# One decoder layer on one core: TensorE, ScalarE and VectorE in a written order from the first norm into the up projection, with a new first stage

## The chip, the cores and the metric

The kernel runs on 1 core of a Trainium2 chip. The metric is the device time of one execution in microseconds (us). A core has five engines that run side by side, each through its own list of instructions in order: PE (TensorE, matrix products), DVE (VectorE, elementwise), ACT (ScalarE, activations and copies), POOL (GpSimd, elementwise) and SP (here it only issues DMAs). An instruction waits at the head of its engine's list until what it reads has been written, and everything behind it on that engine waits with it.

## The reference

One layer of a decoder trunk on 1024 prompt tokens and 8 new tokens (1032 rows, width 1024), in float32:

```python
h = rmsnorm(x, w['norm1_w'])
proj = h @ w['w_in']
q_r, f_r, i_r, g_r, z, xbc_r, dt_r = jnp.split(proj, splits, axis=-1)
...
o_a, S_h_new = hgrn2_mix(heads(q), heads(k), heads(i_r.astype(f32)), heads(log_f), S_h.astype(f32))
o_a = rmsnorm(o_a, w['hgrn_norm_w']) * jax.nn.silu(heads(g_r).astype(f32))
...
xbc, buf_s_new = causal_dwconv(xbc_r, buf_s, w['ssm_conv_w'], w['ssm_conv_b'])
xbc = jax.nn.silu(xbc.astype(f32))
...
dt = jax.nn.softplus(dt_r.astype(f32) + w['ssm_dt_bias'].astype(f32))
y, S_s_new = ssd_scan(X * dt[..., None], A * dt, Bh, Ch, S_s.astype(f32))
...
x = x + jnp.concatenate([o_a, y], axis=-1) @ w['w_out']
h = rmsnorm(x, w['norm2_w'])
gate, val = jnp.split(h @ w['w_up'], 2, axis=-1)
gate, buf_f_new = causal_dwconv(gate, buf_f, w['ffn_conv_w'], w['ffn_conv_b'])
x = x + (jax.nn.silu(gate) * val) @ w['w_down']
```

A final norm follows, and all the recurrent and convolution states are written out.

## The kernel before, in words

**Products.** Each float32 operand is split into a rounded high part and the low rest (`wh`, `wl` of a weight, `hh`, `hl` of an activation), and a product is three passes: high by high, low by high, high by low. The input projection runs in jobs of 128 output columns; a job runs over three groups of 344 tokens, each 8 × 3 = 24 products into one of three accumulators of PSUM (`psmm`). A weight tile is read by a DMA into `ws` (512 KB, two buffers), cast to `wh` on ACT and subtracted to `wl` on DVE (`wload`, lines L188 and L189).

**Stages.** First the norm (`first_norm`): ACT squares (L115), root (L117), DVE puts 1/rms on a diagonal `dg` (L119), PE multiplies the token tile `xt` by `dg` into `tp`, which turns it and scales it in one product, ACT evicts the high part (L128) and DVE the low part (L129). Two jobs of the input projection (x8 and x10, the shared B and C) are merged into it, the products for dt follow, then come the other jobs: x0 to x3 and x4 to x7 (columns of x with their causal convolution, `xbc_close`), z0 to z7 (the gate of the state-space group, evicted by ACT as `sz`), and, for eight heads, q, f, i and g (`sg` is the gate's SiLU). Beside the jobs run the state-space scan (`ssd`, 8 chunks for each of two groups, which reads rows of decays from DRAM as `csb` and `ecs` and keeps a state `S`), its 16 decode blocks for the new tokens (`ssm_decode`: reads `Sd`, `Bb`, `Cb`, ACT scales `Sd`, DVE multiplies, POOL multiplies, DVE reduces), and the eight heads. Then the output projection (jobs o8 to o0, in the end by halves of 516 tokens, o4.6.0 for the first half and o0.6.1, o4.6.1 for the second; evictions `x` at L1078), and the up projection. That takes tile pairs of W_up (gate and value) in blocks of a 2 × 2 split with seven products instead of eight (p1 to p7): for each tile, sums of weight quarters are made on POOL (`wt`, L1246) and split (`up_split`, L1265 on ACT and L1266 on DVE), and for each half of the tokens (set 0, set 1) sums of activation blocks are made and split (`set_of`, `put` at L1181 and L1182). Last come the down projection and the final norm.

**Order.** PE's order is written by hand in the blocks `manual_schedule(engines={PE})`, as calls in the program. ACT, DVE, POOL and SP are put in order by the scheduler of the language. Work that goes beside the jobs hangs on PE's steps: `after(n, work)` calls `work` n steps (products) later, `spread(pieces, n)` runs the next piece of a generator each n steps, `drive` runs a stream evenly over the jobs up to a name, `load_ahead(i, 2)` issues the loads of the next two jobs.

Of the kernel before, what the change touches and what calls it, by code (L numbers as in the profile page):

```python
# [16 lines left out]
P = 128  # L17
# [26 lines left out]
        "x5": (UW, 5), "us": (QW, 10), "t": (512, 4)}  # L44
# [6 lines left out]
def hybrid_layer(  # L51
# [54 lines left out]
    def first_norm(tiles, then=()):  # L106

        xs = []
        for i in tiles:
            xt, t0, n = xtm[i]  # L110
            sq = half("xn")
            ss = keep.tile([P, 4], F32, tag="ss", bufs=4, name=nm("ss"))
            dg = tl("z", "dg")[:, :P]
            for i in range(2):
                A.activation(sq[:n], xt[:n, i * 512:(i + 1) * 512], AF.Square, accum_out=ss[:n, i:i + 1])  # L115
            V.tensor_tensor(ss[:n, 2:3], ss[:n, 0:1], ss[:n, 1:2], op=ALU.add)
            A.activation(ss[:n, 3:4], ss[:n, 2:3], AF.Sqrt, bias=epsc[:n], scale=1.0 / DM)  # L117
            V.reciprocal(ss[:n, 3:4], ss[:n, 3:4])
            V.tensor_scalar(dg[:n, :n], ident[:n, :n], ss[:n, 3:4], None, op0=ALU.mult)  # L119
            xs.append((xt, dg, t0, n))  # L120
        for work_ in then:
            work_()
        c0, c1 = xs[0][2], xs[-1][2] + xs[-1][3]
        for k in range(KT):
            tp = bank("tp")
            for xt, dg, t0, n in xs:
                mm(tp[:, t0 - c0:t0 - c0 + n], xt[:n, k * P:(k + 1) * P], dg[:n, :n])
            A.activation(hT_hi[k][:, c0:c1], tp[:, :c1 - c0], AF.Copy, scale=col("n1", k))  # L128
            V.scalar_tensor_tensor(hT_lo[k][:, c0:c1], tp[:, :c1 - c0], col("n1", k),  # L129
                                   hT_hi[k][:, c0:c1].bitcast(F32), op0=ALU.mult, op1=ALU.subtract)  # L130

# [28 lines left out]
    make_identity(nc, ident)  # L160
    epsc = keep.tile([P, 1], F32, name="epsc")
# [18 lines left out]
    def wload(src, kt, m=P, then=None):  # L180
# [6 lines left out]
        def rounded():  # L187
            A.copy(wh[:, :n], ws[:, :n])  # L188
            V.tensor_tensor(wl[:, :n], ws[:, :n], wh[:, :n].bitcast(F32), op=ALU.subtract)  # L189

        if then is None:
            rounded()
        else:
            then.append(rounded)
        return (wh[:, :n].rearrange("p (k m) -> p k m", m=m), wl[:, :n].rearrange("p (k m) -> p k m", m=m))
# [27 lines left out]
    def job(name, load, run):  # L223
        jobs.append((name, load, run))
# [13 lines left out]
    def tick():  # L238
        for item in list(later):
            item[0] -= 1  # L240
            if item[0] <= 0:
                later.remove(item)
                item[1]()
# [9 lines left out]

    def step(last):
# [29 lines left out]
    def w_in(off):  # L284
        return lambda: wload(w_in_[0, :, off:off + P], KT)
# [81 lines left out]

    def xbc_close(j, ext):
        G.tensor_copy(ext[:, 3 + T:3 + T + 32].rearrange("p (b r) -> p b r", r=4)[:, :, 0:3],
                      bufT[:, j, :].rearrange("p (b r) -> p b r", r=3))  # L370
        n = T + 32
        acc = tl("big", "xbc")
        conv_tail(acc, ext, 4, "cw", "cb", j, XT, n)
        A.activation(acc[:, :T], acc[:, :T], AF.Silu)
        A.activation(acc[:, T:NT], acc[:, T + 3:T + 32:4], AF.Silu)
        return acc

    def xbc_job(j, put):
        ext = []
        def begin():  # L380
            ext.append(xbc_open())
            if j in (5, 7):
                spread(ssm_decode(0, (5, 7).index(j)), 16)
# [12 lines left out]

    rounded = []
    first = [(j, wload(w_in_[0, :, OFF_X + j * P:OFF_X + (j + 1) * P], KT, then=rounded), xbc_open()) for j in (8, 10)]
    for i in range(3, 9):
        load_x(i)  # L400
    vec_cols(0)
    for c in range(NCH):
        first_norm(range(3 * c, 3 * c + 3), () if c else rounded)
        for j, w, ext in first:
            xbc_evict(j, ext, c, chunks[c], prod(w, 0, P, hT_hi, hT_lo, chunks[c]))


    ones = keep.tile([P, P], F32, name="ones")
    G.memset(ones, 1.0)
# [9 lines left out]
    bufT = const.tile([P, XT, 24], F32, name="bufT")  # L419
    for _ in conv_state(state_conv_ssm[0].rearrange("b r d -> (b r) d"), 24, XT, bufT):  # L420
        pass
    vec_cols(1)
    vec_cols(2)
    BT[0], CT[0] = (xbc_close(j, ext) for j, w, ext in first)

    wdt_s = tl("ld", "wdt_s")[:, :KT * 16].rearrange("p (k m) -> p k m", m=16)
    wdt = tl("d", "wdt", F32R)[:, :KT * 32].rearrange("p (k m) -> p k m", m=32)
    SP.dma_start(wdt_s, w_in_[0, :, OFF_DT:OFF_DT + 16].rearrange("(k p) m -> p k m", p=P))
    A.copy(wdt[:, :, 0:16], wdt_s)
    V.tensor_tensor(wdt[:, :, 16:32], wdt_s, wdt[:, :, 0:16].bitcast(F32), op=ALU.subtract)  # L430
    dtr = tl("g", "dtr")
# [1063 lines left out]
```

## Time and profile before

| | before |
|---|---|
| runs, us | 1803.27, 1798.18, 1803.65 |
| median, us | 1803.27 |
| span of the profiled execution, us | 1794.6 |
| clock of TensorE, mean over the span | 0.992 of full |

The span reaches from the first to the last instruction of one profiled execution, for which no time of its own is shown beside its span; the runs were timed apart from it. The clock is what the throttle granted TensorE. A product of 344 columns is shown with about 0.32 us, but products overlap: in an undisturbed stretch one starts each 0.157 us.

### The profile page before, as it was taken

Reading aid. Unit: us, or ns where it says so; the run is one execution under the profiler, and the core shown is the slowest. Engines: PE = TensorE matmul, PEld = TensorE weight load, DVE = VectorE, ACT = ScalarE, POOL = GpSimd, SP = SyncE. Lnnn points to the kernel's source line nnn. Section 1 sums busy time; section 2 is a strip of 40 time slices with the busy share of each in tenths; the row PEclk is TensorE's granted clock in tenths of the full one; section 3 lists DMA queues with packets and bytes.
Section 4 is the critical chain, followed back from the end, with each engine's and each line's share of the span. In section 5 each row is a group of like instructions: output and inputs, shape, how many; then the busy total and the mean of one; then the engine's idle time right before and its main releaser. Section 6 shows DMA issues by size and latency. Waiting matters only on the chain.

```text
span 1794.6 us, 38584 instructions
## 1 busy us (share of the span) xinstructions
PE 1741.0 (97%) x16215; PEld 1685.0 (94%) x16215; DVE 1116.6 (62%) x2002; ACT 789.1 (44%) x1414; POOL 409.8 (23%) x415
## 2 busy tenths in 40 slices
PE   7999899999999999999999988999999999999998
PEld 7998798999999999999999978999999999999997
DVE  4658967556555564557746769666666667555545
ACT  6477688454544444345323344333433334111114
POOL 1103331110110110110100364455444542000001
PEclk9999999999999999999999998999999999999999
DMA  5135634553222221235334431222222225422212
GB/s 154 36 98 155 171 100 138 175 147 99 72 77 63 78 79 50 74 96 159 94 107 130 133 116 48 94 73 71 75 85 90 72 71 193 150 95 96 96 60 95
DMA packets 218018, 182.34 MB, mean 102 GB/s; under 512 B 13388, under 2 KB 195158, under 8 KB 217830
## 3 DMA queue, kind: packets, MB, share of 16 engines
q1 hardware_dynamic: 217558, 179.80, 32.5%
q8 instruction: 127, 2.08, 0.5%
q14 instruction: 45, 0.37, 0.1%
q0 software_dynamic: 288, 0.10, 0.0%
HBM read 141.53 MB, written 38.52 MB: 100 GB/s over the span
## 4 chain that ended last, share of the span: by engine, by line
PE 77%; DVE 8%; ACT 6%; DMA 5%; issue 2%; POOL 2%; SPq 0%; DVEq 0%; POOLq 0%; ACTq 0%
PE mm L93 30%; PE ub L93 14%; PE dn L93 13%; PE ua L93 10%; PE a L93 2%; PE o L93 1%; DMA csb<-cs_d 1%; ACT csb L549 1%; PE tp L93 1%; DVE wl L189 1%; DMA Bb<-bc_d 1%; PE kv L93 1%; DMA Sd<-in_state_ssm_dram 1%; DMA out_dram<-Sd 1%; DVE xbc L352 1%
## 5 line engine op out<-in xcount | busy, mean ns | idle before, releaser
L93 PE MATMUL mm<-hh,wh 128*128 128x344 f32 x1248 | 406.2, 326 | 2.6 <-ACT sz L685 2.6
L93 PE MATMUL mm<-hl,wh 128*128 128x344 f32 x1248 | 403.9, 324 | 0.0
L93 PE MATMUL mm<-hh,wl 128*128 128x344 f32 x1248 | 402.8, 323 | 0.0
L93 PEld LDWEIGHTS mm<-hh,wh 128*128 128x128 f32 x1248 | 234.6, 188 | 5.9 <-ACT sz L685 2.9
L93 PEld LDWEIGHTS mm<-hh,wl 128*128 128x128 f32 x1248 | 234.9, 188 | 2.4 <-issue 1.2
L93 PEld LDWEIGHTS mm<-hl,wh 128*128 128x128 f32 x1248 | 234.6, 188 | 2.5 <-issue 0.9
L188 ACT CAST wh<-ws 128x1024 fp32r<-128x1024 f32 x96 | 100.6, 1048 | 265.4 <-PE dn L93 135.8
L93 PE MATMUL ub<-ul,wh 128*128 128x258 f32 x704 | 199.6, 284 | 4.2 <-DVE ul L1182 4.2
L93 PE MATMUL ub<-uh,wh 128*128 128x258 f32 x704 | 201.1, 286 | 2.0 <-ACT uh L1181 2.0
L93 PE MATMUL ub<-uh,wl 128*128 128x258 f32 x704 | 200.8, 285 | 0.0
L93 PE MATMUL dn<-ah,wh 128*128 128x256 f32 (+1 forms) x640 | 180.7, 282 | 1.2 <-DVE x L1425 1.2
L93 PE MATMUL dn<-al,wh 128*128 128x256 f32 (+1 forms) x640 | 180.3, 282 | 0.0
L93 PE MATMUL dn<-ah,wl 128*128 128x256 f32 (+1 forms) x640 | 179.9, 281 | 0.0
L93 PE MATMUL mm<-mh,wh 128*128 128x258 f32 x512 | 148.2, 290 | 10.7 <-DVE x L1078 8.1
L189 DVE TENSOR_TENSOR wl<-ws,wh 128x1024 fp32r<-128x1024 f32 x96 | 125.3, 1306 | 52.5 <-ACT wh L188 52.3
L93 PE MATMUL ua<-ul,wh 128*128 128x258 f32 x528 | 148.9, 282 | 0.9 <-DVE ul L1182 0.9
L93 PE MATMUL ua<-uh,wl 128*128 128x258 f32 x528 | 149.4, 283 | 0.0
L93 PE MATMUL ua<-uh,wh 128*128 128x258 f32 x528 | 149.2, 282 | 0.0
L93 PE MATMUL mm<-ml,wh 128*128 128x258 f32 x512 | 146.5, 286 | 0.0
L93 PE MATMUL mm<-mh,wl 128*128 128x258 f32 x512 | 146.1, 285 | 0.0
L93 PEld LDWEIGHTS ub<-ul,wh 128*128 128x128 f32 x704 | 134.6, 191 | 4.9 <-DVE ul L1182 4.9
L93 PEld LDWEIGHTS ub<-uh,wh 128*128 128x128 f32 x704 | 134.2, 191 | 2.5 <-ACT uh L1181 2.5
(331 smaller groups left out, 3925.0 us busy)
## 6 DMA issues: line engine op xcount, KB each, us to landing
ws<-in_w_in_dram SPq DMA_DIRECT2D x52, 512.0 KB
ws<-in_w_up_dram SPq DMA_DIRECT2D x44, 512.0 KB
ws<-in_w_out_dram SPq DMA_DIRECT2D x24, 512.0 KB
act_d<-val SPq DMA_DIRECT2D x22, 516.0 KB
al<-act_d SPq DMA_DIRECT2D x22, 516.0 KB
ws<-in_w_down_dram SPq DMA_DIRECT2D x22, 512.0 KB
ml<-mix_d SPq DMA_DIRECT2D x48, 172.0 KB
csb<-cs_d SPq DMA_DIRECT2D x32, 256.0 KB
```

The source lines that it names most:

```text
L93: PE.matmul(out, lhsT, rhs, start=start, stop=stop)
L188: A.copy(wh[:, :n], ws[:, :n])
L189: V.tensor_tensor(wl[:, :n], ws[:, :n], wh[:, :n].bitcast(F32), op=ALU.subtract)
L352: V.scalar_tensor_tensor(acc[:, :n], ext[:, q:q + n], col(wname, q * ntile + j), acc[:, :n], op0=ALU.mult, op1=ALU.add)
L549: A.activation(csb3[:, h, :], csb3[:, h, :], AF.Relu, scale=-1.0, bias=cst[:, h0 + h:h0 + h + 1])
```

## The change

- **Order.** From the first norm to the fourth visit of the up projection (`v == 4`), PE, ACT and DVE are all in the written order, the order of the calls; from there PE alone, as before. POOL and SP stay with the scheduler.
- **First stage.** `first_norm` goes. PE turns `xt` with the identity (transposes), the root is taken once for three token tiles, the diagonals `dg` are multiplied by ones into a row `rb` of 1/rms, DVE scales (`normed`, into `hn`), ACT casts `hn` to the high part, DVE subtracts one step later (`low`). The products of x8, x10 and dt follow four transposes behind (`LAG`), the dt products between the others.
- **Weights.** A `Weight` is loaded first and rounded later (`round`), 8 steps into the job before it. Loads go out one job earlier (`load_ahead(i, 3)`).
- **Pieces.** A `Flow` is a generator whose yields say after how many steps the next piece comes; the convolution, the dt chain, the constants, the decode blocks and the squares of the gate are such flows. A decode block issues all its reads at once and uses them 28 steps later.
- **Reads of the scan.** `csb` is fetched a chunk ahead (`ssd_rows`), `ecs` too (`ssd_carry`).
- **Up projection.** Tile 0 of W_up is loaded and split twice: visits are tile 0 for set 0, tile 1 for both, tile 0 for set 1, then the others. The loads of visit 0 are issued after o4.6.0. The order and engine of the set's sums change (the second subtraction moves behind p5, the fourth sum from POOL to DVE).

```diff
+    class Weight:
...
+        def round(self):
+            if self.pair is None:
...
+                A.copy(hi, ws)
+                V.tensor_tensor(lo, ws, hi.bitcast(F32), op=ALU.subtract)
...
+    class Flow:
...
+        def go(self):
+            self.item = None
+            n = next(self.pieces, None)
+            if n is not None:
+                self.item = after(n, self.go)
...
     def step(last):
         tick()
         if at[1] is None:
-            load_ahead(at[0], 2)
-            name, load, run = jobs[at[0]]
-            at[1] = run(loaded[at[0]]) if load is not None else run()
+            i = at[0]
+            load_ahead(i, 3)
...
+            if nxt is not None:
+                after(8, nxt.round)
+            at[1] = run(loaded[i].round()) if load is not None else run()
...
+        def stats(self):
+            ss = self.ss
+            V.tensor_tensor(ss[:, 0:3], self.sq[:, 0, 0:3], self.sq[:, 1, 0:3], op=ALU.add)
+            A.activation(ss[:, 0:3], ss[:, 0:3], AF.Sqrt, bias=epsc, scale=1.0 / DM)
+            V.reciprocal(ss[:, 0:3], ss[:, 0:3])
...
+    def turned(s):
+        g, k = groups[s // KT], s % KT
+        tps[s] = bank("tp")
+        for xt, t0, n in g.tiles:
+            PE.transpose(tps[s][:, t0 - g.c0:t0 - g.c0 + n], xt[:n, k * P:(k + 1) * P], ident[:n, :n])
...
+    def normed(u):
+        g, k = groups[u // KT], u % KT
+        hn = half("hn")[:, :g.w]
+        V.scalar_tensor_tensor(hn, tps.pop(u)[:, :g.w], col("n1", k), g.rows_[:, :g.w], op0=ALU.mult, op1=ALU.mult)
+        A.copy(hT_hi[k][:, g.cs], hn)
+        hns[u] = hn
+        if u:
+            low(u - 1)
...
+                    if i == 0 and c == NCH - 1:
+                        loaded[0].round()
...
+    ordered = ExitStack()
+    ordered.enter_context(tc.manual_schedule(engines={mybir.EngineType.PE, mybir.EngineType.Activation, mybir.EngineType.DVE}))
...
+            got.append((b0, bs, Bb, Cb, Sd))
+        yield 28
+        for b0, bs, Bb, Cb, Sd in got:
             for b in range(4):
                 A.activation(d4(Sd)[:, b, :], d4(Sd)[:, b, :], AF.Copy, scale=ddb[:, 1, j, b0 + b:b0 + b + 1])
             V.tensor_tensor(d4(Bb), d4(Bb), cb(xdd[:, 0, bs]), op=ALU.mult)
-            yield
+            yield 5
...
         for c in range(1, NC):
             yield 2.5
-            ssd_front(g, c, parts)
+            ssd_front(g, c, parts, rows[c])
             yield 2.5
-            ssd_back(parts, c - 1)
+            ssd_back(parts, c - 1, carry_[c - 1])
+            if c + 1 < NC:
+                rows[c + 1] = ssd_rows(g, c + 1)
+            carry_[c] = ssd_carry(g, c)
...
+    VISITS = [(0, (0,)), (1, (0, 1)), (0, (1,))] + [(j, (0, 1)) for j in range(2, FT)]
...
-    with tc.manual_schedule(engines={mybir.EngineType.PE}):
+    if True:
         finish("o4.6.0")
-        after(16, lambda: set_norm(0, 0))
-        after(30, lambda: set_norm(0, 1))
-        after(36, lambda: spread(set_of(0), 9))
+        up_load(0)
+        after(24, lambda: set_norm(0, 0))
+        after(32, lambda: set_norm(0, 1))
+        after(44, lambda: spread(set_of(0), 7))
...
+        for v, (j, inst) in enumerate(VISITS):
+            if v == 4:
+                ordered.close()
+                ordered.enter_context(tc.manual_schedule(engines={mybir.EngineType.PE}))
```

Three places of the engines' lists follow (engine's rows in order; a name's number tells buffers apart; the line numbers are those of each kernel).

PE at the start of the program. Before, where `tp` is a product of the diagonal `dg` with `xt`, and `hh`, `hl`, `wh`, `wl` are high and low parts:

```order
L93 MATMUL tp_201<-dg_154,xt_100 128x128
L93 MATMUL tp_201<-dg_163,xt_102 128x128
L93 MATMUL tp_201<-dg_172,xt_104 128x128
L93 MATMUL mm_231<-hh_81,wh_126 128x344
L93 MATMUL mm_257<-hh_81,wh_132 128x344
L93 MATMUL tp_207<-dg_154,xt_100 128x128
L93 MATMUL tp_207<-dg_163,xt_102 128x128
```

And the same place in the change, where `rb` is the row of 1/rms:

```order
L496 MATMUL tp_194<-ident,xt_100 128x128
L496 MATMUL tp_194<-ident,xt_102 128x128
L496 MATMUL tp_194<-ident,xt_104 128x128
L93 MATMUL rb_198<-dg_179,ones 128x128 x3
L496 MATMUL tp_208<-ident,xt_100 128x128
L496 MATMUL tp_208<-ident,xt_102 128x128
L496 MATMUL tp_208<-ident,xt_104 128x128
L93 MATMUL mm_223<-hh_81,wh_128 128x344
L93 MATMUL mm_224<-hh_81,wh_134 128x344
L93 MATMUL mm_223<-hl_89,wh_128 128x344
```

The diagonals moved from the first operand of every turning to one product of three behind twelve transposes.

DVE at the end of the output projection, as the first set of the up projection is made. Before, with `x` the evictions, `wl` the low parts of weights (of `ws` as loaded, of `wt` from POOL's sums) and `ul` the low parts of the set:

```order
L1078 TENSOR_TENSOR x_1159_9865<-x_1159_9865,mm_12126 128x258
L1266 TENSOR_TENSOR wl_12149<-wt_12083,wh_12148 128x512
L1266 TENSOR_TENSOR wl_12149<-wt_12079,wh_12148 128x512
L1182 TENSOR_TENSOR ul_12165<-sm_12001,uh_12164 128x1032
L1078 TENSOR_TENSOR x_1159_9865<-x_1159_9865,mm_12154 128x258
L1078 TENSOR_TENSOR x_1159_9865<-x_1159_9865,mm_12176 128x258
```

And in the change, from the same part of the weights on (`wt_11751`, `wt_11749`):

```order
L1488 TENSOR_TENSOR wl_12124<-wt_11751,wh_12123 128x512
L1488 TENSOR_TENSOR wl_12124<-wt_11749,wh_12123 128x512
L1294 TENSOR_TENSOR x_1153_9575<-x_1153_9575,mm_12115 128x258
L184 TENSOR_TENSOR wl_12154<-ws_12041,wh_12153 128x1024
L1401 TENSOR_TENSOR ul_12144<-sm_11823,uh_12143 128x1032
L1294 TENSOR_TENSOR x_1179_9900<-x_1179_9900,mm_12141 128x258
L1401 TENSOR_TENSOR ul_12159<-sm_11824,uh_12158 128x1032
L1406 TENSOR_TENSOR sm_11823<-sm_11823,x_1258_10548 128x516
L1406 TENSOR_TENSOR sm_11823<-sm_11823,x_1276_10693 128x516
L1294 TENSOR_TENSOR x_1179_9900<-x_1179_9900,mm_12170 128x258
```

The weight parts still stand ahead of evictions, but the loads they come from are issued after o4.6.0, a pass of the output projection ahead; and the sums `sm` now stand among the evictions.

ACT at the end of the last head, where the gate `sg` is evicted and the output projection's operand `mh` is cast from `ml`. Before:

```order
L1017 CAST mh_9481<-ml_9477 128x344
L1017 CAST mh_9482<-ml_9478 128x344
L1017 CAST mh_9523<-ml_9519 128x344
L1017 CAST mh_9524<-ml_9520 128x344
L826 ACT_TABLE_LOAD
L826 ACTIVATE sg_9305<-mm_9306 128x344
L826 ACTIVATE sg_9305<-mm_9307 128x344
L826 ACTIVATE sg_9305<-mm_9308 128x344
```

And in the change:

```order
L1038 ACT_TABLE_LOAD
L1038 ACTIVATE sg_9340<-mm_9341 128x344
L1038 ACTIVATE sg_9340<-mm_9342 128x344
L1038 ACTIVATE sg_9340<-mm_9343 128x344
L1229 CAST mh_9514<-ml_9510 128x344
L1229 CAST mh_9515<-ml_9511 128x344
L1229 CAST mh_9516<-ml_9512 128x344
L1229 CAST mh_9517<-ml_9513 128x344
```

The casts of the output projection's first operand, twelve in all, moved from ahead of the table load to behind the three gates.

More of the change, by code (lines that the diff above doesn't have):

```diff
@@ L252, in spread, with __init__, finish, prepare @@
         go()
+    class Flow:
+        def __init__(self, pieces):
+            self.pieces, self.item = pieces, None
+            self.go()
+        def go(self):
[3 more added lines that the diff above has]
+                self.item = after(n, self.go)
+        def finish(self):
+            if self.item is not None:
+                later.remove(self.item)
+                self.item = None
+            for _ in self.pieces:
+                pass
+    prepared = set()
+    def prepare(i):
+        if i < len(jobs) and i not in prepared:
+            prepared.add(i)
+            if jobs[i][3] is not None:
+                jobs[i][3]()
     def step(last):
@@ L400, in hybrid_layer @@
+    load_x(3)
+    SP.dma_start(wdt_s, w_in_[0, :, OFF_DT:OFF_DT + 16].rearrange("(k p) m -> p k m", p=P))
+    for i in range(4, 9):
         load_x(i)
     vec_cols(0)
[L402 to L409, printed above, removed]
+    bufT = const.tile([P, XT, 24], F32, name="bufT")
```

663 lines of the change are left out of this document (416 added, 247 removed).

## The prediction

> **What bounds the kernel now.** I read the busy table of the page first, then the busy time by stage, then PE's waits, and last the clock behind them.
>
> ```profile
> PE 1741.0 (97%) x16215; PEld 1685.0 (94%) x16215; DVE 1116.6 (62%) x2002; ACT 789.1 (44%) x1414; POOL 409.8 (23%) x415
> ```
>
> TensorE is busy for 97% of the span. A change that keeps its products can win only what PE waits, what it runs at a low clock, and what it does beyond need. The windows say in which stage that lies (PE busy, then DVE and ACT, then clock):
>
> ```profile
> 0.00:62.00 62.00, 52.13 (x343) 47.81 (x344) 27.47 (x81) 37.64 (x88) 8.74 (x28) 1.00 0.43 128
> 62.00:420.00 358.00, 342.83 (x2527) 320.90 (x2526) 253.46 (x442) 240.23 (x460) 80.04 (x80) 1.00 0.45 131
> 420.00:840.00 420.00, 416.95 (x5313) 396.77 (x5311) 234.81 (x426) 184.40 (x294) 51.95 (x38) 1.00 0.28 81
> 840.00:1130.00 290.00, 273.77 (x2562) 266.36 (x2563) 199.49 (x356) 112.76 (x209) 79.39 (x72) 0.96 0.35 107
> 1130.00:1794.00 664.00, 655.37 (x5476) 653.20 (x5474) 401.38 (x701) 214.06 (x364) 189.67 (x199) 1.00 0.28 94
> ```
>
> PE idles 62.00 − 52.13 = 9.9 us at the start, 15.2 us in the convolution and state-space stage, 3.0 us over the heads, 16.2 us from the output projection into the up projection, and 8.6 us after 1130, most of it the end. The last stage keeps its order, so some 44 us are within reach. The largest of the waits behind the start, over the whole span (us in total, times, longest):
>
> ```profile
> PE mm L93 <- DVE x L1078: 8.1, 5, 6.7
> PE mm L93 <- ACT sz L685: 2.6, 1, 2.6
> PE mm L93 <- ACT sg L826: 2.5, 1, 2.5
> ```
>
> Each is one or a few places where an engine in the middle had something else in hand; none recurs by the dozen. Behind some of them the clock falls to half:
>
> ```profile
> 213.30:216.70 3.40, 3.40 (x19) 0.50 0.67 151
> 841.40:844.80 3.40, 3.40 (x19) 0.50 0.82 265
> 1049.60:1056.40 6.80, 3.09 (x14) 0.50 0.17 47
> 1083.70:1094.00 10.30, 6.07 (x26) 0.50 0.00 1
> ```
>
> At half clock PE loses half of its busy time there: 1.7, 1.7, about 1.5 and 3.0 us, 8 us in all, which the idle columns don't contain.
>
> **The first stage.** Before, PE turns x by products with diag(1/rms), which wait for the whole norm chain; the products for dt follow as a block behind the first two jobs. After, PE turns x with the identity, waiting for x alone, the scale comes in on VectorE, and the dt products stand between the others.
>
> ```profile
> 9.77 2.50 PE L93 MATMUL tp<-dg,xt 128*128 128x128 f32 x10 [3.67 <-DVE dg L119]
> 25.86 4.85 PE L93 MATMUL tp<-dg,xt 128*128 128x128 f32 x42
> 66.00:86.00 20.00, 20.00 (x128) 1.00 0.10 27
> 63.34 1.19 PE L93 MATMUL dps<-sel,dtr 128*128 128x16 f32 x10
> 8.76 0.19 ACT L115 ACTIVATION_READ_ACCUMULATOR xn<-xt 128x1 f32 x1
> 9.86 1.04 ACT L188 CAST wh<-ws 128x1024 fp32r<-128x1024 f32 x1 [0.91 <-DMA ws<-in_w_in_dram]
> L129 DVE SCALAR_TENSOR_TENSOR hl<-tp,vcol,hh 128x384 fp32r<-128x384 f32 (+1 forms) x24 | 13.5, 574 | 12.0 <-ACT hh L128 11.9
> ```
>
> The stage ends before at 63.34. Its 144 products of 344 columns and 48 for dt stay: 192 × 20.00/128 = 30.0 us. A turning record costs 4.85/42 = 0.115 us; there were 144 (a float product takes two), now there are 72 transposes and 9 products of ones with the diagonals: 8.3 and about 2 us. With the small transposes that is 41 us of PE. The first product can't start before the weight cast that begins at 9.86 and ends at 10.9, nor before the chain of the norm, whose square sums end at 8.76 + 0.19 = 8.95 and which then takes a sum, a root, a reciprocal, a diagonal, a product of ones, a copy, a scaling and a cast: eight steps, the longest as long as a row of L129 (0.57), which I estimate at 3.5 us together. So about 12.5 us. Some 15 of the transposes lie ahead of that, so 39 us remain: 51.5. I add 1.7 us for the clock that is low at the start (10 records in 2.50 us above, against 42 in 4.85). At the end, the cast of the first job's weights stands behind the last eviction: a cast of 1.04 and a subtraction of 1.2 us on two engines against 0.8 us of PE left, so 1.5 us of wait. The next job then starts at about 54.5 where it started at 63.3: **−9**. Ends: −5, if VectorE loses 4 us in the first third, where 8 scalings and 8 subtractions of 0.57 and the low parts of two weights and of dt's, some 12.7 us in all, stand against 64 products and 24 transposes and more, 13.4 us of PE; −11, if the seam and the clock cost nothing.
>
> A transpose is not a product, and the Trainium skill speaks against this part: TensorE: Matmul & The Clock Gate, Part 4 (PE-mode transpose), holds that transposing doesn't count as activity for the clock gate as a product does. In this trace transposes stand among products at many places, and the clock of that stage's window is 1.00:
>
> ```profile
> L560 PE MATMUL xp<-ident,xbc x64: 272/273/330, 122.2 to 315.5; 128*128 128x128 f32 x64
> ```
>
> Transposes with little beside them no row shows. What that would do here is a rival below.
>
> **62 to 420 us.** The names on ACT and DVE here, as rows:
>
> ```profile
> ACT csb L549 <- DMA csb<-cs_d: 24.4, 8, 6.7
> ACT Sd L647 <- DMA Sd<-in_state_ssm_dram: 21.0, 7, 5.2
> 374.54 1.28 ACT L647 ACTIVATE Sd<-Sd,ddb 128x128 f32<-128x128 f32 x4 [0.97 <-DMA Sd<-in_state_ssm_dram]
> 377.97 0.40 ACT L647 ACTIVATE Sd<-Sd,ddb 128x128 f32<-128x128 f32 x1 [2.15 <-POOL Cb L652]
> 378.28 0.44 ACT L685 ACTIVATE sz<-mm 128x344 f32<-128x344 f32 x1
> ```
>
> ScalarE sat 45 us in front of instructions whose reads had not landed, with evictions behind them: at 378 it held the eviction `sz`, and PE lost its 2.6 us. After, the `csb` reads go out a whole chunk earlier, both `Sd` reads 28 matmul steps (4.4 us at 0.157) before their first use, and each piece of a decode comes 5 and 11 steps behind the one it depends on. The stage's idle 15.2 us plus 1.7 of clock are 17 us. DVE has 253 us of work in 358 us, ACT 240, so both fit on average; counted along the order written down, DVE has more work than PE in only three or four stretches of 10 us (up to 13 us at the change of stage, 10 to 10.8 around 150 to 190), which three accumulators of 24 matmuls, 3.75 us each, take up. The chains PE itself waits on (`S`, `yd`, `ecs`) keep their lengths, and nothing overtakes now. I leave 5.5 us: **−11.5**. Ends: −15.5 and 0.
>
> **Heads and the seam at 840.** 420 to 840 had 3.0 us idle, 2.5 of it at 840.00:
>
> ```profile
> 835.05 3.13 ACT L1017 CAST mh<-ml 128x344 fp32r<-128x344 f32 x8
> 838.20 1.28 ACT L826 ACT_TABLE_LOAD   x1
> ```
>
> Before, eight casts and a table load stand ahead of the last `sg`; after, the load and the `sg` come first and twelve casts behind them, of which the next group of products needs four: 0.4 for the last `sg`, 4 × 0.39 (3.13/8) and a subtraction of 0.45, 2.4 us again. **0** here (−2 to +2); the heads get **+1** for an order that can't slip by (0 to +12).
>
> **Set 0 of the up projection.** The largest single wait:
>
> ```profile
> 1046.95 0.62 ACT L1265 CAST wh<-wt 128x512 fp32r<-128x512 f32 x1 [5.49 <-POOL wt L1246]
> 1050.04 1.74 DVE L1266 TENSOR_TENSOR wl<-wt,wh 128x512 fp32r<-128x512 f32 x2 [5.29 <-ACT wh L1265]
> 1053.31 0.58 PE L93 MATMUL mm<-mh,wh 128*128 128x258 f32 x1 [6.75 <-DVE x L1078]
> ```
>
> The low part `wl` stood on DVE ahead of the evictions `x`, and waited through ACT for a POOL sum whose load was late. After, the same tile's loads go out a whole pass earlier, so this block goes. PE's idle time around it, and around set 1 behind it:
>
> ```profile
> 1015.00:1062.00 47.00, 39.07 (x303) 37.94 (x302) 37.96 (x58) 20.18 (x33) 22.92 (x21) 0.93 0.42 124
> 1062.00:1100.00 38.00, 29.98 (x209) 27.94 (x208) 32.68 (x50) 15.81 (x28) 16.87 (x15) 0.87 0.05 15
> ```
>
> Here 7.9 us and 1.5 of clock, 9.4. What is late next is DVE itself. Between the end of the pass and the last part of the set stand 7 evictions `x`, 4 halves and 2 whole weight parts, 2 `ul` of 516 columns and 4 of 1032, and 4 `sm`, at these rows (busy, mean ns):
>
> ```profile
> L1078 DVE TENSOR_TENSOR x<-x,mm 128x258 f32<-128x258 f32 x34 | 13.7, 412 | 6.8 <-PE mm L93 6.8
> L1171 DVE SCALAR_TENSOR_TENSOR x<-x,vcol,n2r 128x516 f32<-128x516 f32 x16 | 13.7, 885 | 0.1
> L1182 DVE TENSOR_TENSOR ul<-sm,uh 128x1032 fp32r<-128x1032 f32 x8 | 10.2, 1301 | 0.0
> L1182 DVE TENSOR_TENSOR ul<-x,uh 128x516 fp32r<-128x516 f32 x12 | 9.6, 803 | 0.0
> L189 DVE TENSOR_TENSOR wl<-ws,wh 128x1024 fp32r<-128x1024 f32 x7 | 9.6, 1365 | 0.6 <-ACT wh L188 0.6
> L1266 DVE TENSOR_TENSOR wl<-wt,wh 128x512 fp32r<-128x512 f32 x8 | 8.3, 1064 | 5.5 <-ACT wh L1265 5.5
> L1189 DVE TENSOR_TENSOR sm<-x,x 128x516 f32<-128x516 f32 x4 | 2.7, 680 | 0.0
> ```
>
> That is 2.9 + 4.3 + 2.7 + 1.6 + 5.2 + 2.7 = 19.4 us; many of these means hold time beside POOL, and I take 17, against 7 groups of 12 products at 0.12 us (the last stage above, 655.37 us for 5476), 10 us of PE. Two spare accumulators cover 2.9 us, so some 4 us of wait are left. **−5**; ends −9 and −2.
>
> **Set 1.** Before, 8.0 us idle and 3.0 of clock, 11. After, tile 0 is visited twice with tile 1 between, so the set is due 336 products behind v0's start instead of 84: 336 × 0.12 us is 40 us of PE. DVE has in that stretch 17 weight halves, 8 scalings, 6 + 3 `ul`, 6 `sm`, 6 pieces of the norm and the evictions, by the means above 48 us. It is late by 8 us at the far end, in two or three places, with some clock. **−4**; ends −8 and +3. The second visit's extra 1 MB of loads and its splits are in these 17.
>
> **Sum.** −9 − 11.5 + 0 + 1 − 5 − 4 = −28.5, so a span of 1794.6 − 28.5 = 1766.1. The median of the runs, 1803.27, lies 8.7 us above the profiled span; with that, **1775 us**.
>
> **Rivals.** (1) Nearly all goes: no wait over 1 us left before v4; −11 − 15.5 − 9 − 8 = −43.5, so 1760 us. For it: each wait has a cause that the change addresses. Against: the DVE counts of the two sets. (2) The order in hand gives back what it wins: a wait that a free engine slipped past now holds everything behind it, and 62 to 420 comes out even, with set 1 at 0: 1775 + 11.5 + 4 = 1790. For it: ACT needs 240 and DVE 253 of 358 us with 45 us of ACT waiting on reads. Against: the reads are earlier. (3) The first stage stays at half clock over its first third, 13.4 us of PE: +13, so that the stage gives nothing: 1788. For it: three transposes stand beside every four products; against it, the 64 transposes above. (4) Slower: the 16 decode blocks. Each holds ACT until its `Sd` reads have landed; the longest wait before was 5.2 us, the cover is 4.4 us plus what two accumulators give, 7.5 us. From reads later than about 12 us on, a block costs PE what the one at 378 did, 2.6 us, with 1.7 of clock: 4.3 us; in twelve of the sixteen that is 52: 1775 + 52 = 1827. For it: reads at 131 GB/s in this stage already; against: 12 us is over twice the longest wait. (5) It doesn't do what it says: the lists of the three engines read as written, so this is only that POOL and SP, still ordered as before, set the pace, and set 0's −5 alone is left: 1798.
>
> **Chances.** The forecast, 1766 to 1785: 0.47; (1) 0.20; (2) 0.16; (3) 0.05; (4) 0.06; (5) 0.06. The low end takes in (1) with its ends, 1755; the high end takes in (2) and (3) with room: 1797. What a measurement of this kernel can tell from no change is about 0.3%, 5.4 us. Faster by more than that: 0.47 + 0.20 + 0.16 + 0.05 and a third of (5), 0.90; within: 0.04; slower: 0.06.
>
> **What would show it.** The first transposes at 5 to 9 us and the first 344-column product at 12.5; the next job at 54 to 55 (over 58: the first part is wrong). PE's idle time in what was 62 to 420 at 4 to 7 us, with ACT's waits on `csb` and `Sd` reads under 15 us in place of 45. No clock at half in that stage. No wait of PE over 3 us on `x`; waits of 1 to 3 us on evictions just behind the last pass of the output projection, and on `wl` or `uh` at the third and fourth visit. The forecast is wrong if waits on `sz`, `xbc` or on the heads' tiles come up by the dozen: then an engine in order is the bound, and (2) or (4) holds.

## The result, and the profile after

The change makes the kernel slower: 1855.79 us (median of 4 runs, 1855.23 to 1856.85) against 1801.54 us, a ratio of 1.0313 with a 95% interval of 1.0294 to 1.0331. The prediction was 1775, 1755 to 1797, and had the wrong sign. The profiled execution has a span of 1854.1 us (1794.6 before).

The busy table of the changed kernel, and its windows cut where the same products of PE stand as at 62, 420, 840 and 1130 us before:

```profile
PE 1761.5 (95%) x16161; PEld 1700.0 (92%) x16161; DVE 1143.1 (62%) x2029; ACT 777.7 (42%) x1408; POOL 400.3 (22%) x418
...
0.00:61.00 61.00, 49.71 (x289) 42.24 (x290) 29.20 (x72) 31.22 (x76) 8.80 (x28) 0.97 0.36 113
61.00:450.00 389.00, 352.42 (x2524) 330.01 (x2522) 257.61 (x457) 233.25 (x455) 75.25 (x80) 0.97 0.42 123
450.00:871.60 421.60, 418.70 (x5316) 398.54 (x5315) 239.84 (x420) 179.99 (x283) 51.77 (x38) 1.00 0.26 76
871.60:1187.30 315.70, 284.34 (x2563) 275.30 (x2564) 214.76 (x381) 118.72 (x230) 70.73 (x72) 0.94 0.35 108
1187.30:1853.50 666.20, 656.37 (x5475) 653.95 (x5474) 401.67 (x701) 214.47 (x365) 193.78 (x201) 1.00 0.28 94
```

PE does 54 products fewer and is busy 20.5 us longer, and it idles 92.6 us in place of 53.6. Both come from the second and the fourth stage. In the second, idle time went from 15.2 to 36.6 us and busy time from 342.8 to 352.4 at a clock of 0.97 in place of 1.00; in the fourth, from 16.2 to 31.4 us idle and from 273.8 to 284.3 busy. The heads, which hold nearly a quarter of the span, are 1.6 us longer, the last stage 2.2. DVE has hardly more work than before in the second stage (257.6 us against 253.5), and ACT has less.

PE's waits in the changed kernel (us in total, times, longest), to hold against the list before:

```profile
PE mm L93 <- DVE x L1294: 10.2, 8, 3.4
PE xp L763 <- DVE ecs L791: 6.8, 4, 3.1
PE ua L93 <- ACT wh L1487: 6.2, 2, 5.7
PE vps L123 <- DMA vrows<-in_norm_w_dram: 5.9, 1, 5.9
PE dps L93 <- DVE dps L657: 4.5, 1, 4.5
PE yd L93 <- DVE bt L755: 3.7, 1, 3.7
PE ms L93 <- DVE vd L1056: 3.6, 1, 3.6
...
PE n2ms L93 <- POOL n2r L1310: 3.5, 2, 3.2
PE ua L93 <- DVE wl L1488: 3.5, 2, 2.8
```

The one block of 6.75 us is gone; in its place stand 14 waits of 2.4 to 5.7 us, eleven of them for DVE (behind the first `vps`, which both kernels wait for; before, seven were over 2 us). The clock shows the second half of the cost (the first two rows are for the part on the first stage below):

```profile
14.00:30.00 16.00, 13.71 (x82) 11.97 (x82) 11.89 (x28) 9.69 (x25) 0.00 (x0) 1.00 0.52 165
30.00:47.00 17.00, 16.53 (x111) 13.94 (x109) 8.18 (x19) 9.07 (x25) 0.00 (x0) 1.00 0.03 9
...
71.00:74.40 3.40, 3.33 (x16) 3.36 (x16) 0.00 (x0) 0.00 (x0) 0.00 (x0) 0.50 0.20 57
74.40:78.00 3.60, 3.60 (x15) 3.51 (x15) 3.10 (x5) 0.35 (x1) 0.00 (x0) 0.50 0.00 0
```

Behind the wait of 4.5 us that ends at 71.1 PE runs at half clock for 7 us, of which half is lost: a wait of 4.5 us costs 8.

Who waits for whom between ACT and DVE in the second stage (all engines' waits, 61 to 450 us):

```profile
DVE wl L184 <- ACT wh L183: 40.7, 20, 10.5
...
DVE csb L768 <- ACT csb L760: 27.2, 20, 2.2
ACT sz L903 <- DVE xbc L896: 24.0, 14, 4.3
ACT xbc L410 <- DVE xbc L407: 21.0, 10, 3.9
```

ACT's waits on `csb` and `Sd` reads, 45 us before, are out of this list, as forecast. DVE's wait on `wl` was 4.8 us before, and ACT's waits on `xbc` for `sz` and for `xbc` were 15.5 and 5.2 us. The two engines now wait for each other. One place where it reaches PE, by the timeline (start and duration in us, instruction, idle time before it and its releaser), ACT first, then DVE, then PE:

```profile
160.37 1.27 ACT L404 ACTIVATE xbc<-ext,vcol 128x1056 f32<-128x1056 f32 x1 [0.58 <-DVE last L392]
161.54 1.03 ACT L183 CAST wh<-ws 128x1024 fp32r<-128x1024 f32 x1
...
160.18 0.16 DVE L392 COPY last<-mm 128x11 f32<-128x11 f32 x1
162.60 1.23 DVE L184 TENSOR_TENSOR wl<-ws,wh 128x1024 fp32r<-128x1024 f32 x1 [2.27 <-ACT wh L183]
163.74 1.31 DVE L407 SCALAR_TENSOR_TENSOR xbc<-ext,vcol,xbc 128x1056 f32<-128x1056 f32 x1
164.97 0.68 DVE L791 TENSOR_TENSOR ecs<-yo,ecs 128x512 f32<-128x512 f32 x1
...
165.71 0.66 PE L763 MATMUL xp<-ident,xbc 128*128 128x128 f32 x4 [3.06 <-DVE ecs L791]
```

DVE stands 2.27 us in front of `wl` because ACT has a convolution piece ahead of the cast; then it does `wl` and a convolution piece, 2.4 us, and only then `ecs`, which frees the bank that PE waits for. Neither `wl` nor the convolution was urgent.

### The profile page after: what moved, and what is told of

Same layout as the page of the kernel before. It is cut to its first block, busy times and chain, and to the rows that moved or that the text cites. A ratio compares the mean times of both kernels' runs of the same rounds, so it can differ in the third digit from the quotient of the medians.

```text
span 1854.1 us, 38555 instructions
## 1 busy us (share of the span) xinstructions
PE 1761.5 (95%) x16161; PEld 1700.0 (92%) x16161; DVE 1143.1 (62%) x2029; ACT 777.7 (42%) x1408; POOL 400.3 (22%) x418
## 5 line engine op out<-in xcount | busy, mean ns | idle before, releaser
L93 PE MATMUL mm<-hh,wh 128*128 128x344 f32 x1248 | 411.9, 331 | 1.0 <-ACT wh L183 0.7
L93 PEld LDWEIGHTS mm<-hl,wh 128*128 128x128 f32 x1248 | 238.5, 191 | 5.8 <-DVE hl L500 3.3
L93 PE MATMUL ua<-uh,wh 128*128 128x258 f32 x528 | 153.6, 291 | 7.3 <-ACT wh L1487 6.2
L93 PE MATMUL ua<-ul,wh 128*128 128x258 f32 x528 | 152.8, 289 | 0.9 <-DVE ul L1401 0.9
L93 PEld LDWEIGHTS ub<-uh,wl 128*128 128x128 f32 x704 | 133.3, 189 | 2.9 <-DVE wl L1488 2.8
L184 DVE TENSOR_TENSOR wl<-ws,wh 128x1024 fp32r<-128x1024 f32 x74 | 90.8, 1226 | 66.1 <-ACT wh L183 66.0
```

Of the source, the lines that this page charges most:

```text
L93: PE.matmul(out, lhsT, rhs, start=start, stop=stop)
L184: V.tensor_tensor(lo, ws, hi.bitcast(F32), op=ALU.subtract)
```

## The experiments

All times are beside runs of the kernel before on the same chip. To see where in the program a kernel gains or loses, the same products of PE are counted off in two traces and their starts subtracted (computed from the traces; one profiled execution each, so the last row differs from the ratio by some us; e1 to e15 are the experiments below):

| PE's product at, before, us | after | e11 | e14 | e8 | e10 | e9 |
|---|---|---|---|---|---|---|
| 76.8 (x0) | +9.1 | +0.1 | −0.0 | +0.9 | +2.2 | +0.6 |
| 279.0 (z jobs) | +27.8 | +18.6 | +12.0 | −2.2 | −1.8 | −2.6 |
| 840.0 (output projection) | +31.6 | +13.7 | +8.9 | −0.1 | +1.6 | −5.2 |
| 909.7 | +38.8 | +20.5 | +16.3 | +0.6 | +3.6 | −5.3 |
| 1007.1 | +38.5 | +20.2 | +16.0 | +1.2 | +7.3 | −1.6 |
| 1044.9 | +50.9 | +33.3 | +28.3 | +10.1 | +7.4 | −1.4 |
| 1098.8 (up projection) | +41.2 | +23.5 | +18.5 | −7.0 | −0.2 | −9.3 |
| 1129.0 | +57.2 | +39.5 | +34.5 | +8.4 | −0.1 | −9.3 |
| 1786.8 (end) | +59.3 | +41.6 | +36.9 | +9.9 | +2.6 | −9.6 |

**e1: the orders of ACT and DVE taken back.** All other edits stay; ACT and DVE are scheduled again behind the first stage.

```diff
+        ordered.close()
+        ordered.enter_context(tc.manual_schedule(engines={mybir.EngineType.PE}))
         Flow(dt_pieces())
```

> The changed kernel, with PE alone in the written order from the end of the first stage on; ACT and DVE go back to the scheduler there, all other edits stay. Theory 'order' (the time is lost because ACT and DVE, in strict order, wait for each other with ready work behind them): the 57 us that the changed kernel loses behind 63 us go, and the time comes to 1790 to 1805 us. Rival 'edits' (the first stage, the two visits of tile 0 and the moved reads cost it): 1840 to 1860 us, and the same waits of PE remain.

Measured: 1820.52 us, ratio 1.012 (1.0093 to 1.0146). It lies between the two: the orders of ACT and DVE cost 35 us of the loss, and the other edits some 20.

**e2: the kernel before, its calls as the order of all three engines** from the jobs x0 to x3 to the up projection's tile 3.

```diff
-    with tc.manual_schedule(engines={mybir.EngineType.PE}):
+    with tc.manual_schedule(engines={mybir.EngineType.PE, mybir.EngineType.Activation, mybir.EngineType.DVE}):
...
```

> The kernel before, with ACT and DVE put into the order of the calls as well, from the first state-space job to the third tile of the up projection, none of the other edits. Theory 'order': slower than before by more than the change, since nothing in its code spreads work for three engines in order, 1870 to 1950 us. Rival 'edits': 1795 to 1815 us, as before.

Measured: 1882.5 us, 1.0466 (1.0433 to 1.05). The order alone costs 84 us there, 63 of them up to the product at 279. The calls of the kernel before were placed for PE alone; placed as in the change, the orders of ACT and DVE cost 35.

**e3, e4: one engine at a time.** Behind the first stage, {PE, ACT} in order with DVE scheduled (e3), and {PE, DVE} with ACT scheduled (e4).

```diff
+        ordered.enter_context(tc.manual_schedule(engines={mybir.EngineType.PE, mybir.EngineType.Activation}))   # e3
+        ordered.enter_context(tc.manual_schedule(engines={mybir.EngineType.PE, mybir.EngineType.DVE}))          # e4
```

> The changed kernel with PE and ACT in the written order behind the first stage, DVE left to the scheduler. Theory 'order', the two engines waiting for each other: freeing one breaks the chain in part, 1805 to 1835 us. Rival 'DVE alone' (the order of the busier engine is the whole loss): 1790 to 1805 us. Rival 'edits': 1840 to 1860 us.

> The changed kernel with PE and DVE in the written order behind the first stage, ACT left to the scheduler. Theory 'order', the two engines waiting for each other: 1805 to 1840 us. Rival 'DVE alone': 1845 to 1860 us, as the change. Rival 'edits': 1840 to 1860 us too.

Measured: e3 1823.47, 1.0138 (1.0105 to 1.0171); e4 1851.51, 1.0294 (1.0255 to 1.0333). Freeing DVE takes away 32 us, freeing ACT 4. Of the two orders, it is DVE's that costs.

**e5: more room between `wh` and `wl`.** The low part is handed out 36 products behind the high part, everywhere.

```diff
-                after(8, nxt.round)
+                after(8, nxt.high)
+                after(44, nxt.round)
```

> The changed kernel, all three orders, with one thing moved: a weight's low part (wl, DVE) is handed out 36 products behind its cast (wh, ACT) instead of right behind it. In the changed kernel's trace DVE sits 40.7 us (20 times, longest 10.5) in front of such a wl. Theory 'neighbours' (an order loses where two engines' dependent instructions stand side by side, and wl behind wh is the largest such pair): DVE's wait on wh falls below 12 us and the time falls by 8 to 20 us, to 1836 to 1848 us. Rival 'amount' (DVE simply has too much to do): under 4 us of change.

Measured: 1895.03, 1.0525, 40 us slower, a miss. Its list of PE's waits says why:

```profile
PE mm L93 <- DVE wl L188: 39.9, 17, 3.8
```

In the heads, a run of DVE's operations of the head's norm stands in front of `wl`, and 28 products (4.4 us) ahead of the need were too few: PE waits there six times, 19.7 us. From the product at 420 to the one at 840 the loss grows from +29.1 to +66.7, where the changed kernel's goes from +30.9 to +31.6. Up to the z jobs it did help (+23.8 at 279 against +27.8).

**e6: a bank cleared early.** DVE's memset of `dps`, for which PE waited 4.5 us, stands ahead of the pause in the dt chain.

```diff
-        yield 14
         dps = bank("dps", "nx")
         V.memset(dps[:, 128:NDT], 0.0)
+        yield 14
```

> The changed kernel, all three orders; only DVE's clearing of the bank for the dt sums (dps) moves 14 products ahead, out from behind two convolution pieces and a weight's low part. Theory 'neighbours': the 4.5 us wait of PE at 71 us and the half clock behind it (12 us of it) go, 5 to 10 us in all, 1846 to 1851 us. Rival 'amount': the wait moves to the next step of the dt chain (cps), under 3 us of change.

Measured: 1850.1, 1.0275, as expected. The place at 76.8 went from +9.1 to −0.2, but a part came back one job later (+8.3 at 88.9, where the changed kernel has +14.6). This place is one of DVE's written order: in e1, with DVE scheduled and the memset where it was, it stands at +0.2.

**e7: the early load alone, in the kernel before.** Tile 0 of W_up is loaded behind o4.6.0, with buffers of its own for the gate half.

```diff
+        up_load(0)
         after(16, lambda: set_norm(0, 0))
```

> The kernel before with one idea of the change and none of its orders: the loads of the up projection's first tile go out behind o4.6.0, the gate half in two pieces of its own buffers. Theory 'late load' (the 6.75 us block of before at 1046 hangs on these loads alone): it goes, with its clock, 7 to 12 us: 1787 to 1795 us. Rival 'DVE is the bound there': the sets and evictions take its place, under 4 us: 1795 to 1801 us.

Measured: 1794.76, 0.9975 (0.9962 to 0.9988). The block of 6.75 us is gone; some 4 us come back in the output projection, where the scheduler put `wl` earlier.

**e8: e1 with two places of PE's order mended.** The product `cps` of the dt chain comes 46 products later, and `vd`, which held a bank that the gate's norm shares, gets another.

```diff
-        yield 24
+        yield 70
...
-        dps = bank("vd", "nx")
+        dps = bank("vd")
```

> The kernel of the first experiment (PE alone ordered behind the first stage) with two places of PE's written order mended: cps stands 46 products later, and the transpose vd takes another PSUM bank than the norm sums ms. Theory 'places' (what is left of the loss without the orders of ACT and DVE is PE standing at a few steps that the change put too early): the waits cps 6.8 and ms 8.3 us go with their clock, 14 to 20 us, 1800 to 1807 us. Rival 'edits elsewhere': under 6 us, 1815 to 1821 us.

Measured: 1806.35, 1.0035 (1.0022 to 1.0049), as expected: 14 us for two places of PE's order.

**e9: e7 with the scan's reads a chunk ahead**, as in the change, in the kernel before.

```diff
-            ssd_front(g, c, parts)
+            ssd_front(g, c, parts, rows[c])
...
+            if c + 1 < NC:
+                rows[c + 1] = ssd_rows(g, c + 1)
+            carry_[c] = ssd_carry(g, c)
```

> The kernel of experiment 7 (before, with the early load of the first up tile), and the second idea of the change without its orders: the scan's rows csb and ecs are read one chunk ahead. Theory 'reads cost' (the 45 us that ScalarE waited for reads were what PE lost in the state-space stage): 5 to 12 us faster than experiment 7, 1783 to 1790 us. Rival 'reads were covered' (the scheduler let PE's work pass those waits; the waits of PE there, sT, yo, yd, hang on VectorE): within 3 us of experiment 7, 1792 to 1798 us.

Measured: 1792.51, 0.9953 (0.9932 to 0.9974), in between. It has the lowest median of all, and two small parts of the change make it. What the reads add to e7 is 2 us by the medians and 4 by the ratios, within the intervals. It does not tell what all of ACT's 45 us of waiting cost PE, for 33.6 of them remain in e9's trace: 13.8 on `csb` (24.4 before) and 19.8 on `Sd`, whose reads this edit leaves where they were.

**e10: e8 with the transition into the up projection of e7** in place of the new set and the two visits of tile 0 (the diff is the change's last part taken back).

> The kernel of experiment 8 (new first stage, flows, early reads, two PE places mended, PE alone ordered) with the end taken from experiment 7: sets, visits and timing of the kernel before, with the early load. Theory 'the two visits and the new set order cost': the 8 us that experiment 8 loses between o12 and the third visit go and the early load gives its 7, 1790 to 1796 us. Rival 'they don't': 1801 to 1808 us.

Measured: 1799.49, 0.9989 (0.9977 to 1.0001). It lies between the two. From 1007.1 on it gains as expected (it goes from +7.3 to +2.6, e8 from +1.2 to +9.9), but 6 us are lost ahead of that.

**e11: all three orders, with the mended places** (e6 and e8 in the changed kernel).

> The changed kernel with all three orders, and the places mended that experiments 6 and 8 showed: dps cleared early, cps 46 products later, vd in another bank. Theory 'places and orders add up': 5.5 + some 8 for cps, csT and ms, 1838 to 1846 us, so that some 35 us of ordering ACT and DVE remain. Rival 'the orders only hurt at these places': 1806 to 1825 us.

Measured: 1839.61, 1.0208 (1.0178 to 1.0237), as expected. Beside e8, which has the same calls except that `dps` is cleared where it was, and which lacks the orders of ACT and DVE, it is 33.3 us slower by the medians, 31 by the ratios.

**e12: e10 with ACT in order too**, up to o4.6.0.

> The kernel of experiment 10 with ACT in the written order too, from the first stage to the output projection's second half. Theory 'DVE's order is the whole loss of the orders': within 5 us of experiment 10, 1788 to 1800 us. Rival 'any second order costs': 10 us or more above it.

Measured: 1797.8, 0.9982 (0.9969 to 0.9994). Up to there, with DVE scheduled, ACT's order costs nothing.

**e13, e14, e15: what in DVE's order costs it.** All three start from e11. e13 moves DVE's multiplication of `csb` by `bt` from right behind ACT's exponential to behind the next piece of the scan; e14 also hands out `wl` 20 products behind `wh`, in x and z jobs only (in e11 `wl` stands right behind `wh`, both 8 products into the job); e15 hands out the up projection's close in three pieces.

```diff
+    def ssd_mask(parts, c):
...
+            ssd_mask(parts, c)
             ssd_back(parts, c - 1, carry_[c - 1])
```

```diff
-                after(8, nxt.round)
+                after(8, nxt.high)
+                after(28 if name[0] in "xz" else 8, nxt.round)
```

```diff
+        if v < 4:
+            Flow(up_closing(v, u))
...
+        yield 40
...
+        yield 12
```

> The kernel with the three mended orders (1839.6), with VectorE's two multiplications of csb by bt, which wait for ScalarE's exponential in the written order, handed out a place later, behind the back part of the chunk before. Theory (VectorE's order costs because dependent instructions of two engines stand next to each other, and what TensorE needs stands behind them): the wait of csb for ScalarE (27.2 us, 20 times, in the changed kernel) falls to under 10 us and the state-space stage's loss by 8 to 15 us, 1825 to 1832. Rival (VectorE has simply too much to do in these stretches, in whatever order): less than 3 us, 1837 to 1843.

> As the run before, and the low part of a read weight (wl), which waits for ScalarE's wh, handed out 20 products behind wh in place of 8, in the jobs of the x and z channels alone. Theory: the wait of wl for wh falls there and another 4 to 6 us go. Rival: less than 2 us.

> The kernel with the three mended orders (1839.6), with the close of the first four visits of the up projection (convolution, SiLU, product) handed out in three pieces along the following products, 40 and 12 products apart, in place of one piece. Theory (dependent instructions side by side): the wait of the products for ScalarE's wh at visit 3 (5.7 us in the changed kernel) goes, with the half clock behind it, 1831 to 1834. Rival (amount of work beside GpSimd): less than 3 us, 1837 to 1843.

Measured: e13 1839.69, 1.0212 (1.016 to 1.0263), a miss: DVE's wait on `csb` fell from 27.2 us to

```profile
DVE csb L772 <- ACT csb L760: 4.5, 3, 2.2
```

and the time did not move. Other waits of DVE took part of its place (for `sz` 12.9 us in place of 4.5, on `wl` 70.7 in place of 64.5). Behind `csb`, then, came little that PE needed soon; this is concluded from the time and was not followed further. e14 1833.12, 1.0175 (1.0125 to 1.0225): 6.6 us less than e13 (two runs each, which don't overlap), nearly all of it in this stage. At the product at 247.4 e11 stands at +8.7, e14 at +0.2 and e8, with DVE scheduled, at −4.3. In the next 32 us e14 loses 11.8 and e11 9.9. Where PE first waits there, e14's timeline has ACT, then DVE, then PE:

```profile
258.22 0.49 ACT L911 ACTIVATE sz<-xbc 128x344 f32<-128x344 f32 x1 [4.37 <-DVE xbc L904]
258.62 1.03 ACT L181 CAST wh<-ws 128x1024 fp32r<-128x1024 f32 x1
259.55 0.26 ACT L759 COPY bt<-bg 128x128 f32<-128x128 f32 x1
...
255.13 1.77 DVE L777 TENSOR_TENSOR csb<-csb,bt 128x512 f32<-128x512 f32 x2
257.68 0.51 DVE L904 TENSOR_TENSOR xbc<-xbc,sz 128x344 f32<-128x344 f32 x1
259.84 0.29 DVE L760 TENSOR_TENSOR bt<-bg,tri 128x128 f32<-128x128 f32 x1 [1.66 <-ACT bt L759]
...
260.19 1.15 PE L93 MATMUL yd<-csb,xdt 128*64 128x128 f32 x14 [3.73 <-DVE bt L760]
```

ACT stands 4.4 us in front of the gate's `sz`, for which DVE has pieces of the scan and of the decode ahead of `xbc`; the copy of `bt` stands on ACT behind `sz` and a cast, DVE waits for that copy, and PE waits 3.7 us for DVE's `bt`. The clock is 0.50 for 3.4 us behind it. The changed kernel and e11 have the same wait (3.7 us each), e8 doesn't. Another wait of 3.3 us, for the gate's `gacc`, follows at 287 us. e15 1836.22, 1.0192 (1.0138 to 1.0247), 3.4 us less than e11, between the two and within the intervals: the wait of 5.7 us for `wh` went, and another took most of its place, in

```profile
PE ua L93 <- DVE wl L1488: 7.2, 2, 4.3
```

where e11 has 3.5 us. So dependent neighbours are most of the order's loss up to 247 us, 8.5 of 13.0, but up to 840 us they are shown for 4.8 of 13.8 only. Behind 840 us, where e11 loses some 18 us more than e8, they are shown for 3 of them. In all, moving such neighbours gave back some 10 of the 33 us (6.5 in e14, 3.4 in e15, which were not run together). How the rest splits between other neighbours and DVE's amount of work (35.9 of 37.8 us busy from 1007.1 to 1044.9 already before) stays open; that the chain at 260 us is one of them is read from the trace and wasn't tried.

## Why the prediction was wrong

**The ladder.** From 1855.8, three places mended (e11) give −16.2, two in PE's order (`cps` and the bank of `vd`) and one in DVE's (the clearing of `dps`); the orders of ACT and DVE taken off (e8) −33.2; the old transition into the up projection (e10) −6.9. That is 1799.5, where the kernel before is 1801.5.

**The step that failed** is the one for 62 to 420 us, −11.5: "counted along the order written down, DVE has more work than PE in only three or four stretches of 10 us […], which three accumulators of 24 matmuls, 3.75 us each, take up". The stage came out 32 us longer (from −1.1 at the next job to +30.9 at 420). The step counted amounts of work on one engine. The amounts were right (257.6 us of DVE in 389), but an engine in order stands: it waits for the other engine with PE's next operand behind it, however much time it has over the stage. Of the 31.6 us lost by the product at 840, 13.8 are the orders of ACT and DVE (e11 against e8), of which e3 and e12 put next to nothing on ACT's; 5.0 are the clearing of `dps`, one more place of DVE's order (e6); and 12.9 are `cps` of the dt chain and the bank of `vd` (e6 against e11), which I hadn't priced: the sentence "the chains PE itself waits on (`S`, `yd`, `ecs`) keep their lengths, and nothing overtakes now" left out the chains whose place in PE's order the change moved. That DVE's order costs is shown by the runs; that it does so by standing in front of ACT is seen in the traces at single places (165 us above, 260 us in e14), and shown by a run for 4.8 of the 13.8. The sign to look for was in the prediction ("waits on `sz`, `xbc` … by the dozen") and came up: 14 and 10 times on ACT, where the kernel before has 10 and 5.

**Reads.** The forecast of the waits held: ACT's 45 us of waits on reads fell to 1.0. A part of that is ACT coming later, for in e8, with the same reads and ACT scheduled, 19.3 us remain. The gain was not seen: in e9 the reads together with the early load give 9 us, of which the early load alone gives 4.5.

**First stage, −9.** It came out at −1.1: the next job starts at 63.3, and before it started at 64.4, behind ten `dps` products from 63.34 on (1.0 us), which I took for the job and which the change does later. On equal work nothing was won. The first product came at 13.8, not 12.5. PE was busy 45.8 us from there, where I had 39 and 1.7 for the clock. Of the 5.1 us over, 1.7 are a low clock at 48.0 to 51.4 us, three blocks of `cst` products that I had left out are 1.0, and the transposes from 38 us on were dearer than I had them:

```profile
34.86 0.49 PE L496 MATMUL tp<-ident,xt 128*128 128x128 f32 x3
35.10 0.40 PE L93 MATMUL mm<-hh,wh 128*128 128x344 f32 x1
35.34 0.32 PE L93 MATMUL mm<-hl,wh 128*128 128x344 f32 x1
...
38.59 0.54 PE L496 MATMUL tp<-ident,xt 128*128 128x128 f32 x3
39.06 0.42 PE L93 MATMUL mm<-hh,wh 128*128 128x344 f32 x1
39.32 0.32 PE L93 MATMUL mm<-hl,wh 128*128 128x344 f32 x1
```

From start to start, three take 0.47 us there, where I had 0.345, and the product behind them 0.26 in place of 0.157. In some eight such groups that is 1.8 us. In the groups ahead of 37 us they take 0.24 and 0.24, no more than I had; why the later ones take longer is not shown. And 3.7 us were idle, not 1.5. The rival of a low clock under transposes, 1788, fell: from 13.8 to 17.3 us products started 0.29 us apart, at the low clock that I had priced for the start (the trace's first record of the clock is at 17.3, and the window above prints 1.00 ahead of it too), and from there to 48.0 us the granted clock was 1.00. The Trainium skill (TensorE: Matmul & The Clock Gate, Part 4: PE-mode transpose) has transposes not count as activity for the clock as products do; with four or more products between each three of them the trace shows no loss by it up to 48.0 us. What lowered the clock from 48.0 to 51.4 is not shown.

**Heads +1 and the seam 0** held: +1.6 and −1.8 (the first product of the output projection, counted from the last job ahead of it). Behind it, from 840 to 909.7, another 7.2 us went, for which the sum had no term; e11 loses 6.8 there and e8 0.7, so this too is the orders' cost.

**Set 0, −5, and set 1, −4.** Two forecasts held: the block of 6.75 us went (e7 shows the load alone does it), and waits on evictions `x` and on `wl` and `wh` at the third and fourth visit came. They are larger. From 960.8 to 1129.0 the changed kernel loses 18.5 us where I had it win 9. e8, with DVE scheduled, still loses 8 from 960.8 on, and e10, with the old set and visits, wins 7 there. So 10.6 of the 18.5 are the orders' cost, and the new sets and visits themselves cost 15 us beside the old ones (e8 against e10), where −5 and −4 had priced them as a win. DVE's rows behind visit 2, then ACT's and PE's:

```profile
1160.79 2.83 DVE L1488 TENSOR_TENSOR wl<-wt,wh 128x512 fp32r<-128x512 f32 x2
1164.25 0.42 DVE L1545 TENSOR_TENSOR val<-us,ua 128x258 f32<-128x258 f32 x1 [0.63 <-POOL us L1524]
1164.59 4.46 DVE L378 SCALAR_TENSOR_TENSOR fcv<-fext,vcol,fcv 128x1048 f32<-128x1048 f32 x2
...
1169.14 1.06 ACT L1587 ACTIVATE fext<-fcv 128x1024 f32<-128x1024 f32 x1 [7.05 <-DVE fcv L378]
1170.46 1.14 ACT L1487 CAST wh<-ws 128x512 fp32r<-128x512 f32 x2
...
1171.13 0.58 PE L93 MATMUL ua<-uh,wh 128*128 128x258 f32 x1 [5.68 <-ACT wh L1487]
```

ACT stands 7 us in front of the close of a visit whose result goes to DRAM, with the next weights behind it. I had counted DVE's work in this stretch and left out that ACT stands with it. What in the new sets and visits costs the 15 us was not taken apart.

**Rivals.** (4) had the sign, and not the cause: the `Sd` reads left ACT's list of waits. (2), that the order gives back what it wins, had the cause of the orders' share and stopped at even.

## What to carry to other kernels

An order written down for an engine is priced by its waits, not by its work alone: for each instruction that waits for another engine, look at what stands behind it and who needs that. How far apart to put producer and consumer depends on the place: 20 products of PE between `wh` and `wl` won 6.6 us in the x and z jobs (e14), and 36 everywhere cost 40, since `wl` then came too late in the heads (e5). Here the scheduled DVE was worth 33 us over the written one, and ACT's order cost nothing (e12), so take such a change engine by engine and keep the parts that stand alone (the early load and the reads ahead, 0.9953). Look too at what PE itself is ordered to do too early: two places gave 14 us (e8).

## What the runs showed of the hardware

DVE's operations with two inputs in SBUF took up to twice as long beside POOL. The pair `wl` takes 1.29 us with POOL idle, and 2.83 us (the `wl` at 1160.79 above) with POOL at work on `wt` and `val`, by the changed kernel's timeline:

```profile
1152.99 1.29 DVE L1488 TENSOR_TENSOR wl<-wq,wh 128x512 fp32r<-128x512 f32 x2
...
1160.64 1.28 POOL L1468 TENSOR_TENSOR wt<-wt,ws 128x512 f32<-128x512 f32 x1
1161.88 1.18 POOL L1523 TENSOR_TENSOR val<-us,us 128x258 f32<-128x258 f32 x1
```

The Trainium skill (GPSIMD Engine Reference, section 1, Specifications) has GpSimd's SBUF interfaces shared with VectorE's where a VectorE instruction has two SBUF inputs, as `wl` has; the rows agree. Over the whole trace (computed from it, medians) one `wl` of 128x512 from `wt` takes 0.69 us with POOL idle (26 of them) and 1.12 with POOL busy for over nine tenths of it (61), while an eviction `x` of 128x258, which reads one of its inputs from PSUM, takes 0.42 either way (79 and 10).

A wait of PE can cost more than its length: behind 4.5 us at 71 us the clock stood at 0.50 for 7 us. Over the whole span PE was busy 20.5 us longer than before with 54 products fewer, against 39 us of added idle time.
